# Up projection: the first 256 columns of u and g on tokens 0 to 255 first, the last 128 tokens afterwards with tokens stationary

## The chip, the cores and the metric

The kernel runs on one core of one Trainium2 chip. The metric is the device time of one execution in microseconds (us), lower is better; the time before is the median of three runs.

## The reference

One layer of a hybrid trunk: adaptive layer norm, a mixer of retention and mLSTM heads, its output projection, a post-norm, and then a feed-forward block with a convolution over tokens. It works on 384 tokens (128 of a prompt, 256 of a latent grid whose rows are 64 wide), with a model width of 2048 and a feed-forward width `D_FF` of 5504. All values are float32. The part around the change:

```python
x = _ln(ALPHA * x + g1 * mix) * ln1_g + ln1_b      # mix = heads @ w_out
h = _ln(x) * (1.0 + sc2) + sh2
...
ug = h @ w_up                                      # (tokens, 2 * D_FF)
u, g = ug[..., :D_FF], ug[..., D_FF:]
ffn = (silu(_seq_conv(u, conv_ff, grid)) * g) @ w_down
...
x = _ln(ALPHA * x + g2 * ffn) * ln2_g + ln2_b
```

`_seq_conv` takes, for each column, a weighted sum over three neighbouring tokens, within the prompt or within a grid row. g2 is one of six modulation vectors, each a product of a conditioning vector with a slice of `w_mod`.

## The kernel before, in words

**Arithmetic.** Every float32 operand of a product is split into two fp32r parts, hi (a cast on ACT, L117) and lo (source minus hi, on DVE or POOL, L118). A product is three matmuls: hi·hi, hi·lo, lo·hi. Tokens come in three tiles of 128: tile 0 is the prompt, tiles 1 and 2 the latent grid. The width of 2048 is 16 k-tiles.

**The stages around the change.** The output projection `w_out` is done in four blocks of 512 columns. The last block goes token tile by token tile, each followed by `norms(tt)`: residual, post-norm (DVE, L945 and L947, 128x2048 each), statistics (bn_stats, L1027), the negative scaled mean nm (L927, with a power on POOL that gives brs), and the normalised rows xn on ACT (L1033; for tile 2 the rows lie in the buffer l1g, for tile 0 in g1b). Then `h2_piece(tt, kt)` turns a 128x128 piece of xn by a PE transpose (L114, tile xtp), scales and shifts it to h (ACT L1048 for single pieces of tiles 0 and 1, DVE L1050 else) and splits it: ah on ACT, al on POOL (single pieces of tiles 0 and 1) or DVE. After five k-tiles, tiles 1 and 2 go together, as pieces of 256 tokens.

The up projection has the columns stationary and the tokens moving: `mm_a` (L182 to L184) multiplies a 128x128 block of weights with all 384 tokens, N = 384. It works on 256 columns at a time, first of u, then of g; the product's sums are the PSUM tiles psu. The first u product runs inside the stage of the h2 pieces, two pieces behind; the first g product is `up_product(pmm, 1, 0, 2)`. `up_gate` then makes the gated activation: ACT writes y = u times the middle convolution weight (L1120, scale from cfw), DVE adds the two outer taps from u in PSUM (`conv_taps`, four instructions L345 and L349 for each 128 columns), ACT applies silu (L1122), DVE multiplies by g (L1123), and the result is split into fah and fal for the down projection.

cfw holds the convolution's weights. They are loaded by POOL's DMA queue as rows (cfr, L1097), transposed on PE (pcf) and copied on DVE (cfw, L1102). The last modulation vector, g2's, is accumulated on DVE in the feed-forward stage: for each of 16 k-tiles and each half, SP loads 128x1024 weights (mraw, L234, three buffers) and DVE does a pair of instructions on macc (L283 for the first k-tile, L286 after), one for each conditioning vector.

**What sets the order.** The framework schedules every instruction from dependencies and its own estimates, and fixes for each engine and each DMA queue one order, which the engine follows in order. Buffers come from pools, and later pools take over the space of earlier ones; an instruction that writes a buffer waits for the last reader of what lay there before. Weights go through four raw buffers (SP, L141), and three hi and lo buffers each. PSUM has eight banks: five of pool pmm and three of pool pat in the stage of the change, and from the third product on eight of pool pps, in the same space. The next u product (columns 256 to 511) thus reuses banks of the stage before.

Of the kernel before, what the change touches and what calls it, by code (L numbers as in the profile page):

```python
# [9 lines left out]
F32 = mybir.dt.float32  # L10
F32R = mybir.dt.float32r
# [4 lines left out]
P = 128  # L16
D = 2048
KT = D // P
LP = 128
LS = 256  # L20
T = LP + LS
# [61 lines left out]
def hybrid_step(ctx, tc, ca, cb, x_prompt, x_sample, state_ret, state_c, state_n, state_m, c, c_ctx,  # L83
# [74 lines left out]
    def weights_a(w2, k0, nk, c0, nc_=256, perm=False):  # L158
        src = w2[k0 * P:(k0 + nk) * P, c0:c0 + nc_].rearrange("(k p) n -> p k n", p=P)
        return weights([(lambda r: r[:, :nk * nc_].rearrange("p (k n) -> p k n", k=nk), src)], nk * nc_, perm)  # L160
# [18 lines left out]
    def mm_a(ps, w, kk, width, m, ah, al, start, stop):  # L179
        hi, lo = w  # L180
        s = slice(kk * width + m * P, kk * width + (m + 1) * P)
        nc.tensor.matmul(ps, lhsT=hi[:, s], rhs=ah, start=start, stop=False)  # L182
        nc.tensor.matmul(ps, lhsT=hi[:, s], rhs=al, start=False, stop=False)  # L183
        nc.tensor.matmul(ps, lhsT=lo[:, s], rhs=ah, start=False, stop=stop)  # L184
# [765 lines left out]
    with ExitStack() as p2:  # L950
        g1p = pool("g1p", 1, p2, reuse_waits="tile")
        sb2 = pool("sb2", 2, p2, reuse_waits="tile")
        g1b = g1p.tile([P, 2, D], F32, name="g1b")
        l1g = g1p.tile([P, D], F32, name="l1g")
        l1b = g1p.tile([P, D], F32, name="l1b")
        for kt in range(KT - 2, KT):
            new_act(kt, mixt[kt])
        mixs.close()
        share_splits(0)
        xnp = pool("xnp", 1, p2, side="right", reuse_waits="tile")  # L960
        wo = w_out[0]
        p2m = ExitStack()
        mp = pool("mp2", 3, p2m, reuse_waits="tile")
        raws4 = mod_loads(lambda: mp.tile([P, 2048], F32, tag="mraw", name="mraw"),
                          [(q, 4, 4 * D + j * 512, 512) for j in range(2 * NV, 4) for q in range(0, KT, 4)], 2)
        mods4 = Stepper(chain(*[mod_tensor(4, 4 * j, 4, pmm, sb2, raws4, 4) for j in range(2 * NV, 4)]), 0.9)

        def residual_loads(nb):
            s = slice(nb * 512, (nb + 1) * 512)
            for tt in range(NT):  # L970
                nc.sync.dma_start(out=r[tt][:, s], in_=tok_rows(x_prompt, x_sample, tt)[:, s])
            for v in range(2):
                nc.sync.dma_start(out=g1b[:, v, s], in_=modrow[2, v:v + 1, s].to_broadcast([P, 512]))

        def w_out_block(nb, ks):
            ps = [(pat if nb == 1 else pmm).tile([P, 512], F32, tag="ps", name="pso") for _ in range(NT)]
            for k0 in range(0, ks, 2):
                part_b(ps, weights_b(wo, k0, 2, (nb * 512,)), 2, k0, 0, KT - 1)
                if nb > 0:
                    mods4.step()  # L980
                if nb < 3 and k0 == 10:
                    residual_loads(nb)
                if nb == 2 and k0 == 14:
                    residual_loads(3)
                if nb == 1 and k0 == 8:
                    mod_from_rows(3, KT, pat, sb2, "sh2", 0.0)
                if nb == 2 and k0 == 6:
                    rows_bcast(l1g, ln1_g, D)
                    rows_bcast(l1b, ln1_b, D)
                if nb == 2 and k0 == 8:  # L990
                    mod_from_rows(4, 8 * NV, pat, sb2, "sc2", 1.0)
            return ps

        for nb in range(3):
            ps = w_out_block(nb, KT)
            for tt in range(NT):
                residual(sb2, g1b, tt, nb, ps[tt], True, True)
        mods4.finish()
        p2m.close()
        wx = pool("wx", 1, p2, reuse_waits="tile")  # L1000
        ps = [pmm.tile([P, 512], F32, tag="ps", name="pso") for _ in range(NT)]
        ws = []
        for i in range(KT // 2):
            raw = wraw.tile([P, 1024], F32, tag="raw", name="raw")
            nc.sync.dma_start(out=raw.rearrange("p (k n) -> p k n", k=2),
                              in_=wo[2 * i * P:(2 * i + 2) * P, 1536:2048].rearrange("(k p) n -> p k n", p=P))
            if i < KT // 2 - 3:
                hi = wx.tile([P, 1024], F32R, name=f"wxh{i}")
                lo = wx.tile([P, 1024], F32R, name=f"wxl{i}")
                split(hi, lo, raw)  # L1010
                ws.append((hi, lo))
            else:
                ws.append(split_weights(raw))
        xn = [None] * NT

        def norms(tt):
            residual(sb2, g1b, tt, 3, ps[tt], True, True)
            if tt == NT - 1:
                mark["pb1"] = mark["pow"]
            st = post_stats(tt)  # L1020
            if tt == NT - 1:
                mark["pa2"] = mark["pow"]
            for s in post_norm(tt, st, l1g, l1b, 1):
                pass
            xst = small.tile([P, 4, 6], F32, tag="bst", name="xst")
            for j in range(4):
                nc.vector.bn_stats(out=xst[:, j, :], in_=r[tt][:, j * 512:(j + 1) * 512])  # L1027
            mv, rs = aggr(xst)
            nm = neg_scaled_mean(mv, rs)
            t = l1g if tt == NT - 1 else g1b[:, 0, :] if tt == 0 else xnp.tile([P, D], F32, tag="xn", name="xn")  # L1030
            for j in range(4):
                s = slice(j * 512, (j + 1) * 512)
                nc.scalar.activation(t[:, s], r[tt][:, s], AF.Identity, bias=nm, scale=rs)  # L1033
            xn[tt] = t

        new_hi, new_lo = [None] * KT, [None] * KT

        def h2_piece(tt, kt, n=1):
            w = n * P
            ps = pat.tile([P, w], F32, tag="ps", name="xtp")  # L1040
            for j in range(n):
                transpose(ps[:, j * P:(j + 1) * P], xn[tt + j][:, kt * P:(kt + 1) * P])
            ts = slice(tt * P, tt * P + w)
            h = sb2.tile([P, 2 * P], F32, tag="h2", name="h2", bufs=5)[:, :w]
            v = min(tt, 1)
            sc, sh = modf["sc2"][:, v, kt:kt + 1], modf["sh2"][:, v, kt:kt + 1]
            if tt < 2 and n == 1:
                nc.scalar.activation(h, ps, AF.Identity, bias=sh, scale=sc)  # L1048
            else:
                nc.vector.tensor_scalar(out=h, in0=ps, scalar1=sc, scalar2=sh, op0=ALU.mult, op1=ALU.add)  # L1050
            if tt == 0:
                new_hi[kt] = acts.tile([P, T], F32R, tag=f"ah{kt}", name=f"ah{kt}")
                new_lo[kt] = acts.tile([P, T], F32R, tag=f"al{kt}", name=f"al{kt}")
            split(new_hi[kt][:, ts], new_lo[kt][:, ts], h, nc.gpsimd if tt < 2 and n == 1 else nc.vector)

        for tt in range(NT):
            for kt in range(KT):
                mm_b(ps[tt], ws[kt // 2], kt % 2, act_hi[kt], act_lo[kt], tt, kt == 0, kt == KT - 1)
                if tt == NT - 1 and kt >= 5:
                    h2_piece(0, kt - 5)  # L1060
            norms(tt)
        for kt in range(KT - 5, KT):
            h2_piece(0, kt)
        for kt in range(5):
            h2_piece(1, kt)
        wu, wd = w_up[0], w_down[0]
        ps_first = [pmm.tile([P, T], F32, tag="ps", name="psu") for _ in range(2)]
        wg = None
        for i in range(KT + 2):
            if i < 5:  # L1070
                h2_piece(2, i)
            elif i < KT:
                h2_piece(1, i, 2)
            if i == KT - 1:
                mark["h2"] = mark["lo"]
            kt = i - 2
            if kt < 0:
                continue
            if kt % 4 == 0:
                if kt < 12:  # L1080
                    with tc.issue_after(mark["pb1"] if kt < 4 else mark["pa2"]):
                        wg = weights_a(wu, kt, 4, 0, 256)
                else:
                    wg = weights_a(wu, kt, 4, 0, 256)
            for m in range(2):
                mm_a(ps_first[m], wg, kt % 4, 256, m, new_hi[kt], new_lo[kt], kt == 0, kt == KT - 1)
        act_hi[:], act_lo[:] = new_hi, new_lo


# [37 lines left out]
            out.append((ah, al))  # L1127
        return out

    a = up_gate(0, ps_first, up_product(pmm, 1, 0, 2))  # L1130
    psum_a.close()
    pps = pool("pps", 8, p3, space=PSUM, reuse_waits="tile")

# [116 lines left out]
```

## Time and profile before

| what | us |
|---|---|
| runs: median of three (lowest, highest) | 2064.02 (2063.2, 2068.23) |
| the profiled execution's own time | 2066.45 |
| its span | 2064.6 |
| PE busy in the span | 1985.1 (96%) |
| DVE busy | 1238.6 (60%) |
| ACT busy | 688.5 (33%) |
| POOL busy | 235.9 (11%) |
| mean granted TensorE clock (share of full speed) | 0.984 |

Busy times are sums over an engine's instructions. The chain is the work that ended last, followed back from the last instruction, each step to what released it. Rows of a timeline give start, duration, engine, line of the kernel, operation and tiles (out<-in), and in brackets the idle time of the engine just before and what ended it. Matmuls are pipelined, so their spacing from start to start, not the duration, tells what one costs. The granted clock (PEclk) is the TensorE clock that the throttle gave, as a share of full speed.

### The profile page before, as it was taken

What the parts mean: (1) busy time and instruction counts of PE and PEld (TensorE: products, weight loads), DVE (VectorE), ACT (ScalarE), POOL (GpSimd) and SP (SyncE); (2) the same over time, 40 slices, a digit from 0 to 9 for tenths busy, and PEclk for the clock granted to TensorE, in tenths of its full rate; (3) what the DMA queues carried; (4) which work ended last, traced back from release to release, by engine and by line L of the source; (5) the groups of instructions that cost most, each with busy time, mean ns of one, the idle gap of its engine ahead of it and who ended that gap; (6) DMA issues with size and microseconds to landing.
All of it is one profiled execution on the core that took longest, in us unless ns stands there. A gap on an engine that the chain in (4) does not pass through costs nothing.

```text
span 2064.6 us, 26331 instructions
## 1 busy us (share of the span) xinstructions
PE 1985.1 (96%) x10233; PEld 1748.3 (85%) x10233; DVE 1238.6 (60%) x1792; ACT 688.5 (33%) x1048; POOL 235.9 (11%) x225
## 2 busy tenths in 40 slices
PE   6999999999989998998999999999999999999995
PEld 4677888898878876777999889999889998999984
DVE  4655798987879744477944323477334444444478
ACT  4223333333333443235233333333222332233331
POOL 0001354222212111022000000000000000000004
PEclk9999999999999999998999999999999999999998
DMA  9895985876877436734744334465334444434342
GB/s 348 262 307 167 183 202 173 257 204 215 197 186 221 142 104 222 278 111 137 246 123 123 125 129 124 123 202 181 123 130 124 123 143 143 127 109 143 113 153 102
DMA packets 260637, 352.30 MB, mean 171 GB/s; under 512 B 16143, under 2 KB 200784, under 8 KB 259360
## 3 DMA queue, kind: packets, MB, share of 16 engines
q1 hardware_dynamic: 256240, 340.08, 55.0%
q0 software_dynamic: 4272, 10.54, 1.5%
q8 instruction: 80, 1.31, 0.3%
q14 instruction: 45, 0.37, 0.0%
HBM read 343.16 MB, written 7.41 MB: 170 GB/s over the span
## 4 chain that ended last, share of the span: by engine, by line
PE 82%; DVE 9%; DMA 3%; issue 3%; SPq 1%; POOL 1%; ACT 1%; POOLq 0%; DVEq 0%; ACTq 0%
PE psu L182 11%; PE psu L184 11%; PE psu L183 11%; PE psd L192 5%; PE psd L191 5%; PE psd L190 5%; DVE macc L286 4%; PE psa L182 3%; PE psa L184 3%; PE psa L183 3%; PE psb L191 3%; PE psb L190 3%; PE psb L192 3%; DMA mraw<-in_w_mod 2%; PE pso L190 2%
## 5 line engine op out<-in xcount | busy, mean ns | idle before, releaser
L118 DVE TENSOR_TENSOR lo<-raw,hi 128x1024 fp32r<-128x1024 f32 (+4 forms) x444 | 486.3, 1101 | 533.4 <-ACT hi L117 533.0
L117 ACT CAST hi<-raw 128x1024 fp32r<-128x1024 f32 (+4 forms) x473 | 434.9, 929 | 941.0 <-PE psu L183 355.7
L183 PE MATMUL psu<-al,hi 128*128 128x384 f32 x1376 | 467.4, 340 | 0.0
L184 PE MATMUL psu<-ah,lo 128*128 128x384 f32 x1376 | 464.2, 339 | 2.7 <-DVE lo L118 2.7
L182 PE MATMUL psu<-ah,hi 128*128 128x384 f32 x1376 | 466.3, 340 | 0.0
L286 DVE SCALAR_TENSOR_TENSOR macc<-mraw,ct,macc 128x1024 f32<-128x1024 f32 x210 | 285.4, 1396 | 16.1 <-DMA mraw<-in_w_mod 16.0
L184 PEld LDWEIGHTS psu<-ah,lo 128*128 128x128 f32 x1376 | 258.8, 188 | 3.0 <-DVE lo L118 3.0
L182 PEld LDWEIGHTS psu<-ah,hi 128*128 128x128 f32 x1376 | 258.9, 188 | 1.9 <-issue 0.8
L183 PEld LDWEIGHTS psu<-al,hi 128*128 128x128 f32 x1376 | 259.0, 188 | 0.2
L192 PE MATMUL psd<-hi,fal 128*128 128x512 f32 (+1 forms) x484 | 192.0, 397 | 0.0
L191 PE MATMUL psd<-lo,fah 128*128 128x512 f32 (+1 forms) x484 | 189.8, 392 | 0.0
L190 PE MATMUL psd<-hi,fah 128*128 128x512 f32 (+1 forms) x484 | 186.7, 390 | 0.0
L182 PE MATMUL psa<-ah,hi 128*128 128x384 f32 x512 | 177.5, 351 | 1.7 <-ACT hi L117 1.7
L184 PE MATMUL psa<-ah,lo 128*128 128x384 f32 x512 | 176.4, 346 | 1.6 <-DVE lo L118 1.5
L183 PE MATMUL psa<-al,hi 128*128 128x384 f32 x512 | 176.4, 345 | 0.0
L191 PE MATMUL psb<-lo,ah 128*128 128x512 f32 x384 | 154.3, 402 | 1.1 <-DVE lo L118 1.1
L192 PE MATMUL psb<-hi,al 128*128 128x512 f32 x384 | 152.8, 398 | 0.0
L190 PE MATMUL psb<-hi,ah 128*128 128x512 f32 x384 | 146.7, 401 | 1.7 <-ACT hi L117 1.7
L182 PEld LDWEIGHTS psa<-ah,hi 128*128 128x128 f32 x512 | 96.7, 190 | 16.8 <-issue 9.1
L191 PEld LDWEIGHTS psd<-lo,fah 128*128 128x128 f32 x484 | 90.9, 188 | 23.2
L190 PEld LDWEIGHTS psd<-hi,fah 128*128 128x128 f32 x484 | 90.9, 188 | 21.1
L192 PEld LDWEIGHTS psd<-hi,fal 128*128 128x128 f32 x484 | 90.9, 188 | 20.6
(301 smaller groups left out, 2241.4 us busy)
## 6 DMA issues: line engine op xcount, KB each, us to landing
raw<-in_w_up SPq DMA_DIRECT2D x168, 512.0 KB, 3.8
mraw<-in_w_mod SPq DMA_DIRECT2D x112, 512.0 KB, 5.0
raw<-in_w_down SPq DMA_DIRECT2D x84, 512.0 KB, 3.6
raw<-in_w_in SPq DMA_DIRECT2D x128, 256.0 KB, 4.6
raw<-in_w_in SPq DMA_DIRECT2D x52, 512.0 KB, 6.5
wm<-in_w_mod SPq DMA_DIRECT2D x20, 1024.0 KB, 9.2
raw<-in_w_out SPq DMA_DIRECT2D x32, 512.0 KB, 4.1
wm<-in_w_mod SPq DMA_DIRECT2D x16, 768.0 KB, 6.8
```

The lines of the kernel that those rows point to most:

```text
L117: nc.scalar.copy(dst_hi, src)
L118: mark["lo"] = (eng or nc.vector).tensor_tensor(out=dst_lo, in0=src, in1=dst_hi.bitcast(F32), op=ALU.subtract).ins
L182: nc.tensor.matmul(ps, lhsT=hi[:, s], rhs=ah, start=start, stop=False)
L183: nc.tensor.matmul(ps, lhsT=hi[:, s], rhs=al, start=False, stop=False)
L184: nc.tensor.matmul(ps, lhsT=lo[:, s], rhs=ah, start=False, stop=stop)
L190: nc.tensor.matmul(ps, lhsT=ah[:, t], rhs=hi[:, s], start=start, stop=False)
L191: nc.tensor.matmul(ps, lhsT=ah[:, t], rhs=lo[:, s], start=False, stop=False)
L192: nc.tensor.matmul(ps, lhsT=al[:, t], rhs=hi[:, s], start=False, stop=stop)
L286: nc.vector.scalar_tensor_tensor(out=acc[:, v, :], in0=raw, scalar=ct[:, kt, v:v + 1], in1=acc[:, v, :], op0=ALU.mult, op1=ALU.add)
```

## The change

Before, the first u product waits piece by piece for h2 of all three token tiles, and the first g product follows as a product of its own. After, both are started together on tiles 0 and 1 alone:

- Four PSUM tiles `early` (u and g, 128 columns each). The loop over 16 k-tiles makes an h2 piece of tile 1 (single, on ACT and POOL) and runs `mm_a` for u and g on 256 tokens, N = 256: 192 matmuls. From k-tile 8 on it also makes two pieces of tile 2 (on DVE).
- The eight weight loads (four groups of four k-tiles, u and g) are kept: five pairs of hi and lo go into the `wx` buffers that held weights of `w_out` (tiles wuh and wul), three into the ordinary hi and lo buffers. The marks that held back the first weight loads (`issue_after`) are gone.
- Tile 2 follows with its tokens stationary: 96 matmuls of 128x128 tokens against 256 columns of weights, N = 256, into the PSUM tile `psl`, first g, then u, the k-groups in the order 3, 2, 1, 0. ACT copies the two results to rows (tile `late`), and four PE transposes put them into the last 128 columns of the `early` tiles.
- `up_gate(0, *early)` follows; the separate first g product is gone.

Lines behind the new code move by 15 (L1123 is then L1138, L1102 is L1117, L1097 is L1112).

```diff
-                hi = wx.tile([P, 1024], F32R, name=f"wxh{i}")
-                lo = wx.tile([P, 1024], F32R, name=f"wxl{i}")
+                hi = wx.tile([P, 1024], F32R, name=f"wxh{i}", tag=f"wxh{i}")
+                lo = wx.tile([P, 1024], F32R, name=f"wxl{i}", tag=f"wxl{i}")
...
-            if tt == NT - 1:
-                mark["pb1"] = mark["pow"]
             st = post_stats(tt)
-            if tt == NT - 1:
-                mark["pa2"] = mark["pow"]
...
-        for kt in range(5):
+        wu, wd = w_up[0], w_down[0]
+        early = [[pmm.tile([P, T], F32, tag="ps", name="psu") for _ in range(2)] for _ in range(2)]
+        ws_up = {}
+        for kt in range(KT):
+            if kt % 4 == 0:
+                for ug in range(2):
+                    raw = wraw.tile([P, 1024], F32, tag="raw", name="raw")
+                    nc.sync.dma_start(out=raw.rearrange("p (k n) -> p k n", k=4),
+                                      in_=wu[kt * P:(kt + 4) * P, ug * DFF:ug * DFF + 256]
+                                      .rearrange("(k p) n -> p k n", p=P))
+                    i = kt // 2 + ug
+                    if i < 5:
+                        hi = wx.tile([P, 1024], F32R, name=f"wuh{i}", tag=f"wxh{i}")
+                        lo = wx.tile([P, 1024], F32R, name=f"wul{i}", tag=f"wxl{i}")
+                        split(hi, lo, raw)
+                        ws_up[kt // 4, ug] = hi, lo
+                    else:
+                        ws_up[kt // 4, ug] = split_weights(raw)
             h2_piece(1, kt)
-        wu, wd = w_up[0], w_down[0]
-        ps_first = [pmm.tile([P, T], F32, tag="ps", name="psu") for _ in range(2)]
-        wg = None
-        for i in range(KT + 2):
-            if i < 5:
-                h2_piece(2, i)
-            elif i < KT:
-                h2_piece(1, i, 2)
...
-            if kt % 4 == 0:
-                if kt < 12:
-                    with tc.issue_after(mark["pb1"] if kt < 4 else mark["pa2"]):
-                        wg = weights_a(wu, kt, 4, 0, 256)
-                else:
-                    wg = weights_a(wu, kt, 4, 0, 256)
+            if kt >= 8:
+                h2_piece(2, 2 * kt - 16)
+                h2_piece(2, 2 * kt - 15)
+            for ug in range(2):
+                for m in range(2):
+                    mm_a(early[ug][m][:, :2 * P], ws_up[kt // 4, ug], kt % 4, 256, m,
+                         new_hi[kt][:, :2 * P], new_lo[kt][:, :2 * P], kt == 0, kt == KT - 1)
+        late = pat.tile([P, 2, 256], F32, tag="ps", name="psl")
+        ts = slice(2 * P, T)
+        for ug in (1, 0):
+            for n, kt in enumerate([kt for kg in (3, 2, 1, 0) for kt in range(4 * kg, 4 * kg + 4)]):
+                hi, lo = ws_up[kt // 4, ug]
+                cols = slice(kt % 4 * 256, kt % 4 * 256 + 256)
+                for a, b in ((new_hi, hi), (new_hi, lo), (new_lo, hi)):
+                    nc.tensor.matmul(late[:, ug, :], lhsT=a[kt][:, ts], rhs=b[:, cols],
+                                     start=n == 0 and b is hi and a is new_hi, stop=n == KT - 1 and a is new_lo)
+        rows = sb2.tile([P, 512], F32, tag="rt", name="late")
+        for ug in (1, 0):
+            nc.scalar.copy(rows[:, ug * 256:ug * 256 + 256], late[:, ug, :])
+        for ug in (1, 0):
             for m in range(2):
-                mm_a(ps_first[m], wg, kt % 4, 256, m, new_hi[kt], new_lo[kt], kt == 0, kt == KT - 1)
+                c0 = ug * 256 + m * P
+                transpose(early[ug][m][:, ts], rows[:, c0:c0 + P])
...
-    a = up_gate(0, ps_first, up_product(pmm, 1, 0, 2))
+    a = up_gate(0, *early)
```

**DVE, tile 1's normalisation.** r_6697 and r_6698 are the residual rows of tiles 1 and 2, xst the statistics of the normalised rows, bmv their aggregate, lo and wul weight splits. Before, from tile 1's post-norm to its nm (the last row):

```order
L947 SCALAR_TENSOR_TENSOR r_6697<-r_6697,brs,l1b 128x2048
L1027 BN_STATS xst<-r_6697 128x6 x4
L118 TENSOR_TENSOR lo<-raw,hi 128x1024
L210 BN_AGGR bmv<-xst 128x2
L118 TENSOR_TENSOR lo<-raw,hi 128x1024
L916 TENSOR_TENSOR rtmp<-pso,g1b 128x512
L198 TENSOR_SCALAR veps<-bmv 128x1
L118 TENSOR_TENSOR lo<-raw,hi 128x1024
L918 SCALAR_TENSOR_TENSOR r_6698<-r_6698,rtmp 128x512
L927 SCALAR_TENSOR_TENSOR nm<-bmv,brs 128x1
```

After, the same stretch begins one weight split earlier; its first twelve rows:

```order
L118 TENSOR_TENSOR wul_7875<-raw,wuh_7874 128x1024
L947 SCALAR_TENSOR_TENSOR r_6697<-r_6697,brs,l1b 128x2048
L118 TENSOR_TENSOR wul_7881<-raw,wuh_7880 128x1024
L118 TENSOR_TENSOR wul_7959<-raw,wuh_7958 128x1024
L118 TENSOR_TENSOR wul_7965<-raw,wuh_7964 128x1024
L1023 BN_STATS xst<-r_6697 128x6 x4
L118 TENSOR_TENSOR wul_8043<-raw,wuh_8042 128x1024
L916 TENSOR_TENSOR rtmp<-pso,g1b 128x512
L118 TENSOR_TENSOR lo<-raw,hi 128x1024
L210 BN_AGGR bmv<-xst 128x2
L918 SCALAR_TENSOR_TENSOR r_6698<-r_6698,rtmp 128x512
L118 TENSOR_TENSOR lo<-raw,hi 128x1024
```

Five weight splits more stand there, ahead of tile 1's nm; a third lo and rows of tile 2 follow before nm itself.

**DVE, the end of the first products.** cfw is the copy of the convolution's weights, macc the modulation vector's accumulation, L345 and L349 the taps. Before:

```order
L283 TENSOR_SCALAR macc<-mraw,ct 128x1024 x2
L1102 COPY cfw<-pcf 128x129
L286 SCALAR_TENSOR_TENSOR macc<-mraw,ct,macc 128x1024 x2
L118 TENSOR_TENSOR lo<-raw,hi 128x1024
L286 SCALAR_TENSOR_TENSOR macc<-mraw,ct,macc 128x1024 x2
L345 SCALAR_TENSOR_TENSOR y<-psu,cfw,y 128x127
L349 SCALAR_TENSOR_TENSOR y<-psu,cfw,y 128x4x63
L118 TENSOR_TENSOR lo<-raw,hi 128x1024
```

After:

```order
L118 TENSOR_TENSOR lo<-raw,hi 128x1024 x3
L283 TENSOR_SCALAR macc<-mraw,ct 128x1024 x2
L286 SCALAR_TENSOR_TENSOR macc<-mraw,ct,macc 128x1024 x2
L1117 COPY cfw<-pcf 128x129
L286 SCALAR_TENSOR_TENSOR macc<-mraw,ct,macc 128x1024 x2
L345 SCALAR_TENSOR_TENSOR y<-psu,cfw,y 128x127
L349 SCALAR_TENSOR_TENSOR y<-psu,cfw,y 128x4x63
L345 SCALAR_TENSOR_TENSOR y<-psu,cfw,y 128x127
L349 SCALAR_TENSOR_TENSOR y<-psu,cfw,y 128x4x63
L286 SCALAR_TENSOR_TENSOR macc<-mraw,ct,macc 128x1024 x2
```

Three lo splits of the next u product's weights now stand ahead of the first macc, and one macc pair more ahead of cfw. Behind the last row come four more tap rows, a macc pair, the two products with g (L1138), a pair, the two fal splits, five macc instructions and the next u's fourth lo split.

**SP's queue, the loads behind the first weights of the up projection.** Before:

```order
L1005 DMA raw<-in_w_out 128x2x512 x8
L141 DMA raw<-in_w_up 128x4x256 x9
L234 DMA mraw<-in_w_mod 128x1024 x3
L141 DMA raw<-in_w_up 128x4x256
L234 DMA mraw<-in_w_mod 128x1024 x2
```

After:

```order
L1005 DMA raw<-in_w_out 128x2x512 x8
L1067 DMA raw<-in_w_up 128x4x256 x8
L141 DMA raw<-in_w_up 128x4x256 x7
L234 DMA mraw<-in_w_mod 128x1024 x11
L141 DMA raw<-in_w_up 128x4x256
```

The first mraw load now stands behind fifteen w_up loads instead of nine, the last of which takes the raw buffer of the next u product's third weights. The buffer of the first mraw lies where wul of the third k-group of u (wul_8043) was, which the late block reads.

On POOL, cfr's load stood ahead of all the al splits and now stands behind all 32 of tiles 0 and 1; its buffer lies where wuh_7958 was, whose last reader has twelve matmuls of the late block behind it. On PE, the transposes of cfr (pcf) stood in the middle of the first products. Now they are the last rows before the next u product, whose matmuls begin with the fourth row from the end here:

```order
L1093 MATMUL psl<-wuh_7874,ah_7716 128x256
L1093 MATMUL psl<-wul_7875,ah_7716 128x256
L1093 MATMUL psl<-wuh_7874,al_7717 128x256
L114 MATMUL psu<-cst,late 128x128 x4
L114 MATMUL pcf<-cst,cfr 128x43 x3
L182 MATMUL psu<-ah_7683,hi 128x384
L183 MATMUL psu<-al_7684,hi 128x384
L184 MATMUL psu<-ah_7683,lo 128x384
L182 MATMUL psu<-ah_7683,hi 128x384
```

The first of these psu matmuls writes the bank of the second column tile of the first u, so it waits for the last tap that reads it (L349), in both kernels.

More of the change, by code (lines that the diff above doesn't have):

```diff
@@ L1063, in hybrid_step @@
             h2_piece(0, kt)
-        for kt in range(5):
-            h2_piece(1, kt)
-        wu, wd = w_up[0], w_down[0]
-        ps_first = [pmm.tile([P, T], F32, tag="ps", name="psu") for _ in range(2)]
-        wg = None
-        for i in range(KT + 2):
-            if i < 5:
-                h2_piece(2, i)
-            elif i < KT:
-                h2_piece(1, i, 2)
[L1074 to L1078, printed above, removed]
-            if kt % 4 == 0:
-                if kt < 12:
-                    with tc.issue_after(mark["pb1"] if kt < 4 else mark["pa2"]):
-                        wg = weights_a(wu, kt, 4, 0, 256)
-                else:
-                    wg = weights_a(wu, kt, 4, 0, 256)
+        wu, wd = w_up[0], w_down[0]
```

## The prediction

> **What bounds the kernel now.** I read the page first, then the table of stretches around the change, then the timelines of PE, DVE, ACT and SP in it, then the DMA view. The chain that ended last is PE's work for the most part:
>
> ```profile
> PE 82%; DVE 9%; DMA 3%; issue 3%; SPq 1%; POOL 1%; ACT 1%; POOLq 0%; DVEq 0%; ACTq 0%
> ```
>
> So a change pays only where PE stands still, and what it adds to PE it costs. The stretches (columns: window, length, PE busy (count), PEld, DVE, ACT, POOL, granted clock, DMA share, GB/s) show where PE stands still: in the first, between the last product of the output projection and the first of the up projection, thirty instructions, all but one transposes, in 19.7 us; the second holds the first u and g products, the third and fourth the u product of columns 256 to 511 (here "the next u").
>
> ```profile
> 922.40:942.10 19.70, 9.33 (x30) 4.57 (x29) 15.95 (x29) 17.61 (x50) 14.78 (x23) 0.63 0.31 95
> 942.10:979.50 37.40, 37.40 (x213) 36.82 (x212) 29.50 (x50) 14.65 (x24) 0.00 (x0) 0.97 0.56 172
> 979.50:992.40 12.90, 12.90 (x74) 12.90 (x74) 12.90 (x14) 4.60 (x7) 0.00 (x0) 1.00 0.73 235
> ...
> 995.00:1000.00 5.00, 4.54 (x17) 4.54 (x18) 5.00 (x5) 0.00 (x0) 0.00 (x0) 0.66 0.85 230
> ```
>
> The timeline of PE has the ends of these stretches (start, duration, engine, line, operation). The first product starts at 942.12, its 192 matmuls (counted by the row of the psu tiles alone) end where the next u starts, at 979.51, without a gap. The next u stands from 992.41 to 995.46 for its fourth lo split on DVE and then runs cold:
>
> ```profile
> 942.12 0.99 PE L182 MATMUL psu<-ah,hi 128*128 128x384 f32 x2
> ...
> 979.51 0.34 PE L182 MATMUL psu<-ah,hi 128*128 128x384 f32 x1
> ...
> 992.41 0.34 PE L183 MATMUL psu<-al,hi 128*128 128x384 f32 x1
> 995.46 0.45 PE L184 MATMUL psu<-ah,lo 128*128 128x384 f32 x1 [2.71 <-DVE lo L118]
> ...
> 999.39 0.34 PE L182 MATMUL psu<-ah,hi 128*128 128x384 f32 x1
> ```
> ```profile
> 942.10:979.50 37.40, 36.95 (x192) 34.67 (x193) 2.86 (x8) 1.17 (x2) 0.97 0.56 172
> ```
>
> **The streaming, part by part.** Warm spacings, start to start, come from these rows: the first two are seven starts of a dense run (six spacings, 1.06 us: 0.1767 us at N = 384), the next two are 23 starts (22 spacings, 2.64 us: 0.120 at N = 256, from the last down product), the last two four transposes (0.11 each).
>
> ```profile
> 957.20 0.34 PE L182 MATMUL psu<-ah,hi 128*128 128x384 f32 x1
> ...
> 958.26 0.34 PE L182 MATMUL psu<-ah,hi 128*128 128x384 f32 x1
> ```
> ```profile
> 2040.17 0.28 PE L191 MATMUL psd<-lo,fah 128*128 128x256 f32 x1
> ...
> 2042.81 0.28 PE L192 MATMUL psd<-hi,fal 128*128 128x256 f32 x1
> ```
> ```profile
> 953.54 0.27 PE L114 MATMUL xtp<-cst,xn 128*128 128x128 f32 x1
> ...
> 953.87 0.27 PE L114 MATMUL xtp<-cst,l1g 128*128 128x128 f32 x1
> ```
>
> Removed: 192 x 0.1767 = 33.9. Added: 192 + 96 matmuls at N = 256, 288 x 0.120 = 34.6. The arithmetic itself costs 0.7. Between them stay about 27 transposes (3.0; the 16 of tile 2 and the 11 of tile 1 that now stand among the matmuls) and a cold start. The clock's price is read off the stall: from 995.46 to 999.39 are 13 spacings, 3.93 us for 13 x 0.1767 = 2.30, so 1.6 lost. The block from first early matmul to last late one is 34.6 + 3.0 + 1.6 = 39.2 us.
>
> The Trainium skill, "TensorE: Matmul & The Clock Gate", section "Wait — 56ns, not 53.3ns?", gives N ÷ 2.4 GHz plus about 2.5 ns for warm back-to-back matmuls, 109 ns at N = 256: by that the 288 would take 31.4 us, and the end would come 3.2 us earlier than below. This trace's 0.120 is for the same operand type and width, so the row decides.
>
> **The head.** The early matmuls need only tile 1's normalised rows, not tile 2's. On DVE three weight splits stand ahead of tile 1's nm before; with the change five more (the wul tiles) do, about 1.2 each by these rows (DVE first, then ACT, which makes the rows from nm):
>
> ```profile
> 921.29 1.21 DVE L118 TENSOR_TENSOR lo<-raw,hi 128x1024 fp32r<-128x1024 f32 x1
> ...
> 922.59 1.16 DVE L118 TENSOR_TENSOR lo<-raw,hi 128x1024 fp32r<-128x1024 f32 x1
> ...
> 924.32 1.22 DVE L118 TENSOR_TENSOR lo<-raw,hi 128x1024 fp32r<-128x1024 f32 x1
> ...
> 926.86 0.41 DVE L927 SCALAR_TENSOR_TENSOR nm<-bmv,brs 128x1 f32<-128x1 f32 x1 [0.46 <-POOL brs L200]
> ...
> 938.00 0.41 DVE L927 SCALAR_TENSOR_TENSOR nm<-bmv,brs 128x1 f32<-128x1 f32 x1 [0.84 <-POOL brs L200]
> ```
> ```profile
> 928.17 2.92 ACT L1033 ACTIVATE xn<-r,nm,brs 128x512 f32<-128x512 f32 x4
> ...
> 938.44 2.93 ACT L1033 ACTIVATE l1g<-r,nm,brs 128x512 f32<-128x512 f32 x4 [0.30 <-DVE nm L927]
> ```
>
> Tile 1's nm becomes 926.9 + 5 x 1.2 = 932.9. From nm to the first product tile 2 takes 942.1 − 938.0 = 4.1 now; tile 1's nm waited 0.9 longer for ACT than tile 2's did (1.3 against 0.4), so the first early matmul is at 932.9 + 4.1 + 0.9 = 937.9, not 942.1. Bounds: 932 if the five splits were hidden, 942 if their loads are late. I take 937.9, since the order on DVE puts all five ahead. The late block then ends at 937.9 + 39.2 = 977.1 instead of 979.5: 2.4 gained. The row copies on ACT and four transposes (0.44 on PE) lie under the wait that follows, at no cost; without that wait they would cost about 1.2.
>
> **The tail: what the next u waits for.** Here the change adds a wait. The weights' third hi and lo buffers are read in the late block until its 60th matmul, 36 before the end: 977.1 − 36 x 0.12 = 972.8. Then the next u's third weights are split, hi on ACT and lo on DVE; I take the lo's 1.2 above for each: 975.2. Only then its raw buffer is free, SP gets past that w_up load, and behind it come all the mraw loads of the modulation vector, the first of which also needs a buffer that the late block reads. Before, they went out at 955. The DMA view has their landing and that of cfr, and POOL's row where cfr is issued:
>
> ```profile
> 955.05 5.96 SPq L234 DMA_DIRECT2D mraw<-in_w_mod  x3
> ```
> ```profile
> mraw<-in_w_mod SPq DMA_DIRECT2D x19, 512.0 KB, 4.5
> ...
> mbt<-in_b_mod POOLq DMA_DIRECT2D x2, 128.0 KB, 2.8
> cfr<-in_conv_ff POOLq DMA_DIRECT2D x1, 64.5 KB, 7.4
> ```
> ```profile
> 916.38 1.91 POOL L1097 DMA_DIRECT2D cfr<-in_conv_ff  x1
> ```
>
> The first mraw goes out at about 975.3 and lands at 979.8; the second, 0.52 MB at the 235 GB/s of the third stretch, 2.2 later, at 982.0. On DVE two macc pairs, which need these two, now stand ahead of the cfw copy, and further pairs between the convolution taps. Each step's price:
>
> ```profile
> 963.40 1.41 DVE L283 TENSOR_SCALAR macc<-mraw,ct 128x1024 f32<-128x1024 f32 x2
> 964.72 0.29 DVE L1102 COPY cfw<-pcf 128x129 f32<-128x129 f32 x1
> 964.92 2.47 DVE L286 SCALAR_TENSOR_TENSOR macc<-mraw,ct,macc 128x1024 f32<-128x1024 f32 x2
> 967.31 1.22 DVE L118 TENSOR_TENSOR lo<-raw,hi 128x1024 fp32r<-128x1024 f32 x1
> ...
> 970.84 0.35 DVE L345 SCALAR_TENSOR_TENSOR y<-psu,cfw,y 128x127 f32<-128x127 f32 x1
> ...
> 971.48 1.22 DVE L118 TENSOR_TENSOR lo<-raw,hi 128x1024 fp32r<-128x1024 f32 x1
> ...
> 977.69 0.48 DVE L349 SCALAR_TENSOR_TENSOR y<-psu,cfw,y 128x252 f32<-128x252 f32 x1
> ...
> 981.60 0.56 DVE L1123 TENSOR_TENSOR y<-y,psu 128x384 f32<-128x384 f32 x1
> ...
> 986.05 0.57 DVE L118 TENSOR_TENSOR fal<-y,fah 128x384 fp32r<-128x384 f32 x1
> ...
> 988.18 6.09 DVE L286 SCALAR_TENSOR_TENSOR macc<-mraw,ct,macc 128x1024 f32<-128x1024 f32 x5
> 994.16 1.24 DVE L118 TENSOR_TENSOR lo<-raw,hi 128x1024 fp32r<-128x1024 f32 x1
> ```
>
> A macc pair is 2.4, cfw 0.2, four tap rows 2 x 0.64 = 1.3 (start to start). From 982.0: pair 984.4, cfw 984.6, pair 987.0, four taps 988.3, pair 990.7, four taps 991.9. The next u's first matmul writes the bank that the last tap reads, so it starts at 992.0. Before, the last tap ended at 978.2, ahead of 979.51, and the bank was free. cfr isn't what binds: its buffer is read until 12 matmuls before the late block's end, so it lands between 975.7 + 2.8 = 978.5 and 975.7 + 7.4 = 983.1, and three short transposes (under 0.4) later cfw could run, before its turn at 984.4. ACT's y lies under the pair behind cfw.
>
> The fourth lo split, for which the next u stands now, comes after a pair (994.3), two L1123 products (995.4), a pair (997.8), two fal splits (998.9), five macc (6.0: 1004.9): it ends at 1006.2. It is needed 12.9 after the start plus 1.6 for the cold clock: 1006.5. The old stall just goes.
>
> **The sum.** Before, the next u ends at 979.5 + 96 x 0.1767 + 2.9 (3.05 less one spacing) + 1.6 = 1001.0. After: 992.0 + 17.0 + 1.6 = 1010.6. Behind that the chain is PE's products one after the other, with no gap in which the delay could be made up, so 9.6 us stay. The profiled execution took 2066.45 (span 2064.6), 2.4 above the median of the runs, 2064.02; the difference carries over: 2076.0 for a profiled execution, and 2064.0 + 9.6 = **2073.6 us**.
>
> The Trainium skill, same page, section "What's actually happening", has the clock halve after an idle window of about 3.4 us. Here the granted clock was 0.66 after a gap of 2.7. By the page's window before's stall would not have cooled PE by itself, and its going would give back 1.6 less, 11.2 in the sum; the row decides.
>
> **The rivals.**
> - *The loads are not held (not slower).* Place: SP's first mraw and POOL's cfr. If their buffers don't bind and both have landed when DVE finishes the third lo at 975.2, then DVE runs 1.3 + 2.4 + 0.2 + 2.4 + 1.3 + 2.4 + 1.3 = 11.3 without a wait, the next u starts at 986.5 and ends at 1005.1: 4.1 more, 2068.1, no difference that counts. It decides at a first mraw landed by 975. For it: SP ran these loads 20 us ahead before. Against: eleven stand behind the w_up loads in SP's order. Chance 0.12.
> - *The stall stays as well.* The fourth lo has 0.3 us to spare. If the mraw loads come at more than 2.4 apart, every macc between waits, and the next u stands twice: 2 to 4 more, 2075.6 to 2077.6. For it: DMA is at 235 GB/s there, and the eleven mraw and five w_up loads of that stage want 8.4 MB, 36 us at that rate. Against: DVE had no gap for a load from 979.5 to 992.4 (12.90 of 12.90 busy). Chance 0.17.
> - *The head does not come earlier (the change does not do what it says).* If the eight early loads or the splits push tile 1's chain to 937, the early matmuls start at 942.1 and everything moves by 4.2: 2077.8. Chance 0.12.
> - *Faster.* It would need the third lo some 16 us earlier, or the taps done before the late block is; nothing in the rows allows that. Chance 0.04.
>
> **How the numbers follow.** My forecast keeps 0.55, with 2070.5 to 2077 as its own range (the head's start 3 us to either side). 0.3% is 6.2 us, about what a measurement of this kernel can tell from no change (the three runs before lie 5.0 apart). Within it: the first rival and a small part of the forecast's low end, 0.14. Faster 0.04. Slower 0.82. The range, 2067 to 2080, takes in the first rival's 2068.1 and both dearer ones; it leaves out the faster case and sums of two dear cases.
>
> **What would show it.** Right: the first early matmul near 938, the late block's end near 977, then PE idle for some 14 us but for seven transposes, its releaser DVE's taps (or cfr's landing for the first part of it); DVE idle before the first macc for DMA mraw; the next u from 992, cold at first, with no gap before its fourth lo. Wrong: a next u that starts before 987; a first early matmul at or after 942; cfr landing after 985; or a gain in a later stage, for which I see no cause.

## The result and the profile after

The changed kernel takes 2082.36 us (median of four runs, 2078.83 to 2084.21), the kernel before 2063.61 (four runs, 2062.69 to 2068.23). That is 18.8 us slower, where 9.6 was forecast and the range ended at 2080. The ratio is 1.0084 (95% interval 1.0064 to 1.0105); it goes by the means of the same runs, 2081.9 and 2064.5, which are 17.4 apart. The profiled execution after has a span of 2081.1, the one before 2064.6.

PE has nearly the same work; its busy time is 1987.3 against 1985.1, and its share of the chain fell. From the page of after:

```profile
PE 1987.3 (95%) x10333; PEld 1751.9 (84%) x10333; DVE 1236.9 (59%) x1792; ACT 693.8 (33%) x1072; POOL 247.3 (12%) x236
...
PE 78%; DVE 11%; DMA 4%; issue 3%; SPq 1%; POOL 1%; ACT 1%; POOLq 0%; DVEq 0%; ACTq 0%
...
L182 PE MATMUL psu<-ah,hi 128*128 128x384 f32 (+1 forms) x1336 | 449.8, 339 | 7.8 <-DVE y L349 7.8
```

Before, PE's idle time among the up projection's matmuls was 2.7 us, for a lo split (L184); now it is 7.8 us ahead of an L182 matmul, and a convolution tap ends it. The stretches (PE busy in the third column) place it: the early and late block, the wait, and the first part of the next u.

```profile
937.00:978.60 41.60, 40.12 (x315) 39.44 (x314) 20.00 (x43) 18.22 (x51) 10.41 (x18) 0.92 0.10 28
978.60:997.70 19.10, 1.48 (x9) 0.80 (x8) 11.54 (x18) 2.35 (x5) 2.09 (x3) 0.66 0.70 211
997.70:1012.40 14.70, 14.63 (x73) 14.67 (x74) 14.70 (x15) 4.77 (x8) 0.00 (x0) 0.87 0.53 174
```

In the middle one PE does 1.5 us of work in 19.1. Its timeline names what it waits for, twice in a row: first for cfr, then for the last tap.

```profile
978.53 0.28 PE L1093 MATMUL psl<-wuh,al 128*128 128x256 f32 x1
979.27 0.72 PE L114 MATMUL psu<-cst,late 128*128 128x128 f32 x4 [0.46 <-ACT late L1097]
989.38 0.55 PE L114 MATMUL pcf<-cst,cfr 43*128 43x43 f32 x3 [9.39 <-DMA cfr<-in_conv_ff]
997.76 0.66 PE L182 MATMUL psu<-ah,hi 128*128 128x384 f32 x1 [7.84 <-DVE y L349]
```

DVE in the same time: it stands for the first mraw (5.10), does two macc pairs, stands again, now for pcf (4.11), and then goes through pair, taps, pair, taps. The last tap starts at 997.15, and PE goes on right behind it.

```profile
975.73 1.23 DVE L118 TENSOR_TENSOR lo<-raw,hi 128x1024 fp32r<-128x1024 f32 x1 [3.02 <-ACT hi L117]
982.05 1.42 DVE L283 TENSOR_SCALAR macc<-mraw,ct 128x1024 f32<-128x1024 f32 x2 [5.10 <-DMA mraw<-in_w_mod]
983.38 2.47 DVE L286 SCALAR_TENSOR_TENSOR macc<-mraw,ct,macc 128x1024 f32<-128x1024 f32 x2
989.96 0.29 DVE L1117 COPY cfw<-pcf 128x129 f32<-128x129 f32 x1 [4.11 <-PE pcf L114]
990.17 2.47 DVE L286 SCALAR_TENSOR_TENSOR macc<-mraw,ct,macc 128x1024 f32<-128x1024 f32 x2
...
993.85 2.47 DVE L286 SCALAR_TENSOR_TENSOR macc<-mraw,ct,macc 128x1024 f32<-128x1024 f32 x2
...
997.15 0.47 DVE L349 SCALAR_TENSOR_TENSOR y<-psu,cfw,y 128x252 f32<-128x252 f32 x1
...
1010.16 1.22 DVE L118 TENSOR_TENSOR lo<-raw,hi 128x1024 fp32r<-128x1024 f32 x1
```

The executions differ by some us ahead of this stage, so times of different kernels are compared from one mark, the start of the last matmul of the output projection (922.24 before, 920.58 after). From it the next u starts at 57.3 before and 77.2 after, and the first down product at 231.4 and 248.6: 17.2 later. From there to the end of the span they take 911.0 and 911.9.

### The profile page after: what moved, and what is told of

It is laid out like the page before. It is cut to its first block, busy times and chain, and to the rows that moved or that the text cites. A ratio compares the mean times of both kernels' runs of the same rounds, so it can differ in the third digit from the quotient of the medians.

```text
span 2081.1 us, 26570 instructions
## 1 busy us (share of the span) xinstructions
PE 1987.3 (95%) x10333; PEld 1751.9 (84%) x10333; DVE 1236.9 (59%) x1792; ACT 693.8 (33%) x1072; POOL 247.3 (12%) x236
## 4 chain that ended last, share of the span: by engine, by line
PE 78%; DVE 11%; DMA 4%; issue 3%; SPq 1%; POOL 1%; ACT 1%; POOLq 0%; DVEq 0%; ACTq 0%
PE psu L183 12%; PE psu L182 12%; PE psu L184 12%; PE psd L192 5%; PE psd L191 5%; PE psd L190 5%; DVE macc L286 4%; PE psa L182 3%; PE psa L183 3%; PE psa L184 3%; PE psb L191 2%; PE psb L192 2%; PE psb L190 2%; PE modps L255 2%; PE pso L190 2%
## 5 line engine op out<-in xcount | busy, mean ns | idle before, releaser
L118 DVE TENSOR_TENSOR lo<-raw,hi 128x1024 fp32r<-128x1024 f32 (+4 forms) x439 | 479.5, 1098 | 537.7 <-ACT hi L117 537.3
L117 ACT CAST hi<-raw 128x1024 fp32r<-128x1024 f32 (+4 forms) x468 | 429.6, 927 | 941.9 <-PE psu L183 356.6
L182 PE MATMUL psu<-ah,hi 128*128 128x384 f32 (+1 forms) x1336 | 449.8, 339 | 7.8 <-DVE y L349 7.8
L183 PE MATMUL psu<-al,hi 128*128 128x384 f32 (+1 forms) x1336 | 451.2, 338 | 0.0
L184 PE MATMUL psu<-ah,lo 128*128 128x384 f32 (+1 forms) x1336 | 448.8, 338 | 0.0
L182 PEld LDWEIGHTS psu<-ah,hi 128*128 128x128 f32 x1336 | 250.2, 188 | 9.8 <-issue 8.8
L183 PEld LDWEIGHTS psu<-al,hi 128*128 128x128 f32 x1336 | 251.3, 188 | 0.1
L184 PEld LDWEIGHTS psu<-ah,lo 128*128 128x128 f32 x1336 | 251.1, 188 | 0.0
L182 PE MATMUL psa<-ah,hi 128*128 128x384 f32 x512 | 177.8, 352 | 1.7 <-ACT hi L117 1.7
L184 PE MATMUL psa<-ah,lo 128*128 128x384 f32 x512 | 176.3, 346 | 1.6 <-DVE lo L118 1.5
L182 PEld LDWEIGHTS psa<-ah,hi 128*128 128x128 f32 x512 | 96.8, 190 | 16.8 <-issue 9.1
```

What stands on the lines that cost most here:

```text
L117: nc.scalar.copy(dst_hi, src)
L118: mark["lo"] = (eng or nc.vector).tensor_tensor(out=dst_lo, in0=src, in1=dst_hi.bitcast(F32), op=ALU.subtract).ins
```

## The experiments

**Theory A**: the loss is PE's wait between the late block and the next u, and the wait has three causes one behind the other: cfr lands late, macc stands ahead of cfw and the taps, and the next u's first matmul needs the bank that the last tap reads. **Theory B**: the loss is work of PE's own (N = 256, the late block, the transposes), and a shorter wait would be made up elsewhere. All kernels change the changed kernel, except the one that changes the kernel before. The medians are set beside those of the kernel before on the same chip, and the ratios go by the means.

| kernel | median | before | ratio, 95% interval | next u from the mark | first down product |
|---|---|---|---|---|---|
| after | 2082.36 | 2063.61 | 1.0064 to 1.0105 | 77.2 | 248.6 |
| macc behind the taps | 2078.03 | 2064.68 | 1.0050 to 1.0080 | 72.1 | 244.4 |
| that, mraw loads held | 2072.25 | 2064.68 | 1.0023 to 1.0051 | 68.8 | 240.7 |
| cfr early | 2070.33 | 2064.68 | 1.0022 to 1.0044 | 65.5 | 237.5 |
| cfr early, macc behind | 2068.94 | 2065.39 | 1.0005 to 1.0023 | 63.7 | 235.5 |
| free banks alone | 2084.09 | 2064.68 | 1.0073 to 1.0107 | 57.9 | 248.6 |
| no wait (all three) | 2071.75 | 2065.39 | 1.0021 to 1.0046 | 58.3 | 237.6 |
| no wait, splits behind nm | 2072.41 | 2065.39 | 1.0021 to 1.0043 | 58.6 | 237.9 |
| no wait, macc later | 2063.64 | 2065.14 | 0.9984 to 1.0002 | 58.2 | 229.1 |
| before, macc behind the taps | 2060.71 | 2065.39 | 0.9972 to 0.9990 | | 226.8 |

**cfr early.** The load goes ahead of the early block, into columns of g1b that are free:

```diff
+        cfr = g1b[:NF, 1, :3 * P].rearrange("f (t p) -> f t p", t=3)
+        nc.gpsimd.dma_start(out=cfr, in_=conv_ff[0].rearrange("t (f p) -> f t p", p=P))
...
-    cfr = sb3.tile([NF, 3, P], F32, tag="y", name="cfr")
-    nc.gpsimd.dma_start(out=cfr, in_=conv_ff[0].rearrange("t (f p) -> f t p", p=P))
```

> After with the load of cfr moved ahead of the al splits of tile 1, into a buffer that is free there (columns of g1b that tile 2's residual has read); in the order this brings cfw and three of the four tap rows ahead of the first macc. Theory A (the loss is PE's wait before the next u: late cfr, macc ahead of cfw and taps): pcf inside the late block, the next u starts at about 984 instead of 997.8, the fourth lo at 998 is in time, the total falls by 13 to 14, to about 2069. Theory B (the loss is PE's own added work, N = 256 and the late block, and the wait would be made up elsewhere): the next u may start earlier, the total stays above 2077.

It came to 2070.33, 12 less than after, close to the 13 to 14 of theory A. These columns had been read long before, so cfr went out at 827.9 already. The next u started 65.5 after the mark, not at about 63: the last tap rows still stood behind the first macc, which waited for its mraw. On DVE, and what PE then waited for:

```profile
985.70 1.41 DVE L283 TENSOR_SCALAR macc<-mraw,ct 128x1024 f32<-128x1024 f32 x2 [0.93 <-DMA mraw<-in_w_mod]
987.03 0.34 DVE L345 SCALAR_TENSOR_TENSOR y<-psu,cfw,y 128x127 f32<-128x127 f32 x1
987.30 0.47 DVE L349 SCALAR_TENSOR_TENSOR y<-psu,cfw,y 128x252 f32<-128x252 f32 x1
```
```profile
987.91 0.66 PE L182 MATMUL psu<-ah,hi 128*128 128x384 f32 x1 [5.71 <-DVE y L349]
```

**macc behind the taps.** Every macc instruction is ordered behind the last tap of the first columns, that of `up_gate(0)`:

```diff
+            mark["tap"] = tap.ins
...
             if f0 >= 4:
-                mods5.step()
+                with tc.issue_after(mark["first"]):
+                    mods5.step()
...
+    mark["first"] = mark["tap"]
```

> After with all macc instructions ordered behind the last tap of the first columns, cfr as late as in after. Theory A: cfr lands where it did, near 989.4, cfw 990, the taps end without macc pairs between them at 993.4, the next u starts there instead of 997.8: 4.4 less, about 2078. If the taps' wait is only what shows and the fourth lo (behind macc) is the true bound, no gain: 2082.

2078.03, 4.3 less, as theory A said. The two macc pairs between cfw and the last tap were gone, so that from cfw to the next u it took 3.8 instead of 7.8; cfr landed only 1.0 earlier from the mark than in after.

**The mraw loads held as well.** On top of the edit before, the first mraw load goes behind one more load of w_up on SP's queue (`mark["ld"]` is the latest such load):

```diff
+            if f0 == 2 and ug == 1 and k0 == 12:
+                mark["ld8"] = mark["ld"]
             if f0 >= 4:
-                with tc.issue_after(mark["first"]):
+                with tc.issue_after(mark["first"]), tc.issue_after(mark["ld8"]):
...
```

> As the kernel with macc behind the taps, and the mraw loads also ordered behind one more w_up load on SP's queue, so that no mraw load is under way while cfr is. Theory A1 (cfr landed after 11.6 us because three mraw loads of 0.52 MB went out 0.3 us before it): it lands within 7.4 us or less, by 985, and the next u starts near 988.5: 9 less, about 2073. Theory A2 (the queue of POOL is slow by itself there): it lands 11 to 12 us after its issue, and the time is that of the kernel with macc behind the taps, about 2078.

2072.25, 10 less than after, and A1 is right. cfr's row in the DMA view (last number: us from issue to landing) of after, of the kernel with macc behind the taps, and of this one:

```profile
cfr<-in_conv_ff POOLq DMA_DIRECT2D x1, 64.5 KB, 11.6
```
```profile
cfr<-in_conv_ff POOLq DMA_DIRECT2D x1, 64.5 KB, 10.5
```
```profile
cfr<-in_conv_ff POOLq DMA_DIRECT2D x1, 64.5 KB, 7.5
```

With three mraw loads under way cfr takes 10.5; in after, where two more go out before it lands (at 983.5 and 985.9), 11.6; with none, 7.5, near the 7.4 of the kernel before. The load is the same in all three, and so is the rest of its company: a w_up load issued 0.7 before it, and two mbt loads behind it on POOL's queue.

**cfr early and macc behind the taps.** Both edits above.

> After with cfr early and all macc behind the last tap of the first columns. In the kernel with cfr early alone the last two tap rows still stood behind two macc instructions that waited for their mraw. Theory A: without these the taps end about 2.4 earlier, the next u starts 63 us after the last output-projection matmul (65.5 with cfr early alone, 77.2 in after, 57.3 before): 2.4 less than with cfr early alone, about 2068, still 3 to 4 slower than before. Theory B (what is left over before is not this wait): no change from 2070.

2068.94; the next u starts at 63.7 from the mark, near the 63 and 2068 expected. What is left of the wait is the path from the late block's end over the row copies, four transposes, ACT's y and eight tap rows to the bank.

**Free banks alone.** The next u's tiles come from the pools of the stage before:

```diff
+    us2 = up_product(None, 0, 2, 2, [p_.tile([P, T], F32, tag="ps", name="psu") for p_ in (pmm, pat)])
     psum_a.close()
...
-            us = up_product(pps, 0, f, m)
+            us = us2 if f == 2 else up_product(pps, 0, f, m)
```

> After with the next u product in two PSUM banks that the taps do not read (the fifth bank of the first pool and one of the second), so that its first matmul waits for no tap; the order also moves its fourth lo ahead of most macc. Theory A: the next u starts right behind pcf, at 989.9, and runs through: 7.9 less, about 2074.5. Theory B: no change beyond 2 us.

Theory A's expectation failed: 2084.09, nothing gained, as theory B had it, though the next u started right behind the late block and stood only 4.7 us for cfr in its midst. The time was taken back further on. The next weights' loads stand behind mraw loads on SP's queue, and these wait for macc, which began as late as in after (61.2 from the mark, 61.5 there). PE stood twice in the second g product, and its first down product began at 248.6 as in after. The second of these waits is for a lo split behind seven macc instructions (PE first, then DVE):

```profile
1016.53 0.69 PE L182 MATMUL psu<-ah,hi 128*128 128x384 f32 x1 [3.87 <-ACT hi L117]
...
1024.48 0.69 PE L184 MATMUL psu<-ah,lo 128*128 128x384 f32 x1 [6.94 <-DVE lo L118]
```
```profile
1014.84 8.45 DVE L286 SCALAR_TENSOR_TENSOR macc<-mraw,ct,macc 128x1024 f32<-128x1024 f32 x7
1023.21 1.21 DVE L118 TENSOR_TENSOR lo<-raw,hi 128x1024 fp32r<-128x1024 f32 x1
```

So the bank is only the wait that shows; behind it DVE's queue is a bound of its own, about as late.

**No wait: all three causes taken away.** cfr early, macc behind the taps, free banks.

> The kernel before this one with the next u in banks that the taps don't read as well, so all three causes of the wait are gone. Theory A: the next u follows the late block without a gap, 58 us after the last output-projection matmul, in time with before (57.3), and before's own stall (3.05 and a cold clock) is not there: 2062 to 2064, no slower than before. Theory B: N = 256, the late block and the transposes cost PE time of their own: 2067 or more.

Missed: 2071.75, not 2062 to 2064. The next u did follow the late block without a gap (58.3 from the mark). But the order now had eight macc instructions ahead of the last lo of the second g product, and PE stood there. PE first, then DVE:

```profile
1010.45 0.34 PE L183 MATMUL psu<-al,hi 128*128 128x384 f32 x1
1017.29 0.69 PE L184 MATMUL psu<-ah,lo 128*128 128x384 f32 x1 [6.50 <-DVE lo L118]
```
```profile
1006.44 9.66 DVE L286 SCALAR_TENSOR_TENSOR macc<-mraw,ct,macc 128x1024 f32<-128x1024 f32 x8
1016.00 1.23 DVE L118 TENSOR_TENSOR lo<-raw,hi 128x1024 fp32r<-128x1024 f32 x1
```

This number alone would have spoken for theory B. The trace shows a wait of the same kind at another place: a lo split behind macc.

**No wait, macc later.** On top of the kernel without the wait, macc is held behind the last tap of the second columns:

```diff
             out += up_gate(f, us, up_product(pps, 1, f, m))
+            if f == 2:
+                mark["first"] = mark["tap"]
```

> As the kernel without the wait (cfr early, macc held, free banks), with macc held behind the last tap of the second columns instead of the first. In the kernel without the wait PE stood 6.84 us for the last lo of the second g product, which stood behind eight macc instructions. Theory A (PE's own work of the change costs little; what is lost is waits for DVE's macc and for cfr): that stall goes with its cold clock (1.6), the first down product begins 229 to 230 us after the last output-projection matmul (231.4 before, 237.6 in the kernel without the wait), 2062 to 2064, no slower than before but slower than the kernel before with macc behind the taps (2060.7). Theory B (the stall moves once more, to a later weight): 2067 or more.

2063.64, ratio 0.9984 to 1.0002: no difference from before. In the next u and the second g product PE waits only once more, for 0.55:

```profile
1006.25 0.44 PE L184 MATMUL psu<-ah,lo 128*128 128x384 f32 x1 [0.55 <-DVE lo L118]
```

Of the 18.8 us nothing is left, and no work of PE was changed; theory B falls as the explanation of the loss. A small rest isn't excluded: the kernel before has a stall of its own, and beside it with that stall removed (the last experiment) the first down product comes 2.3 later here, and the ratios 0.9993 and 0.9981 are some 2.5 us apart, though their intervals overlap.

**No wait, the splits behind tile 1's nm.** Made on the kernel without the wait, to ask whether the five splits cost the head its gain:

```diff
-                        split(hi, lo, raw)
+                        with tc.issue_after(mark["nm1"]) if kt else ExitStack():
+                            split(hi, lo, raw)
...
```

> As the kernel without the wait, and the weight splits of all but the first two early loads ordered behind tile 1's nm on DVE, so that six splits less stand ahead of it. Theory A (the splits delay the head): the first early matmul comes at 12 to 12.5 us after the last output-projection matmul instead of 16.4, the late block ends 4 earlier, 2058 to 2060. Rival (the early block is then paced by tile 1's pieces on ACT and POOL): it starts earlier and ends no earlier, 2062 to 2064.

Neither number came: 2072.41, with the 6.84 us stall of the kernel without the wait still in it, so the place of the first early matmul is what tells. Tile 1's nm came at 928.17, 4.3 from the mark instead of 11.8, but the first early matmul at 17.4 instead of 16.4. The rival of this experiment is nearer: PE waits for tile 1's pieces, ACT's h among them waits for POOL's al splits, and these come one behind the other without a pause. Here is nm of after, then of this kernel, then ACT's h and POOL's splits of tile 0's last and tile 1's first pieces:

```profile
932.34 0.41 DVE L927 SCALAR_TENSOR_TENSOR nm<-bmv,brs 128x1 f32<-128x1 f32 x1 [0.68 <-POOL brs L200]
```
```profile
928.17 0.41 DVE L928 SCALAR_TENSOR_TENSOR nm<-bmv,brs 128x1 f32<-128x1 f32 x1 [0.64 <-POOL brs L200]
```
```profile
939.19 0.46 ACT L1048 ACTIVATE h<-xtp,sh,sc 128x128 f32<-128x128 f32 x1 [1.37 <-POOL al L118]
```
```profile
931.32 2.52 POOL L200 TENSOR_TENSOR brs<-veps,mhalf 128x1 f32<-128x1 f32 x1 [1.29 <-DVE veps L198]
933.82 11.55 POOL L118 TENSOR_TENSOR al<-h,ah 128x128 fp32r<-128x128 f32 x14
```

Fourteen al splits take 11.55. That isn't 0.83 for each: nine of them take about 0.45, as one does with DVE idle (after, 946.14: 0.47), and five take 1.06 to 2.50. A long one stands beside a DVE instruction with two inputs in SBUF, the post-norm here; beside bn_stats, which has one, four take 1.69 (POOL first, then DVE):

```profile
936.65 2.50 POOL L118 TENSOR_TENSOR al<-h,ah 128x128 fp32r<-128x128 f32 x1
...
941.91 1.69 POOL L118 TENSOR_TENSOR al<-h,ah 128x128 fp32r<-128x128 f32 x4
```
```profile
936.22 2.62 DVE L949 SCALAR_TENSOR_TENSOR r<-r,brs,l1b 128x2048 f32<-128x2048 f32 x1
...
941.55 2.46 DVE L1025 BATCH_NORM_STATS2 xst<-r 128x6 f32<-128x512 f32 x4
```

The Trainium skill, "SBUF — State Buffer", section "Who interferes with whom", says that a DVE instruction with two SBUF inputs contends with a GpSimd instruction that reads SBUF, and that the second one blocks until the first is done; the trace agrees, 2.50 beside the post-norm against 0.45 beside bn_stats. That POOL now holds the head is read off these waits; no run without them was made.

**The kernel before, macc behind the taps.** The same hold, nothing else.

> The kernel before the change, with all macc behind the last tap of the first columns and nothing else. Theory A: the fourth lo of the next u no longer stands behind five macc instructions, the stall of 3.05 us at 992.41 and its cold clock (1.6) go: 4.5 less, about 2060. If the stall is only moved to a later weight: 2063 to 2065.

2060.71, ratio 0.9981 (0.9972 to 0.9990): the expected 4.5 came (4.7 by the medians). The idle time of L184, 2.7 us before, is gone from the page:

```profile
L184 PE MATMUL psu<-ah,lo 128*128 128x384 f32 x1376 | 463.2, 339 | 0.0
```

It is the fastest of all, faster than both kernels, and 2.9 faster than the best version with the change.

## Why the prediction was wrong, point by point

The direction was right, and so was the end of the path: PE waits ahead of the next u, the taps release it, and macc stands ahead of cfw and between the taps. The forecast has about half of the loss. The step that failed is that cfr doesn't bind: in the trace cfr, and not the first macc pairs, is what cfw waits for last. The other half of the miss is the block, taken 2.5 us too short and begun 0.8 too early.

- **Head.** Forecast 937.9, which is 15.7 from the mark; measured 936.99, 16.4 from the mark. Right within 0.8, but the reason was incomplete: with six splits fewer ahead of nm the head gains nothing, since POOL's al splits are next late, and slow beside some of DVE's instructions.
- **The block.** Forecast 39.2, measured 936.99 to 978.65: 41.7. The streaming was right (36 matmuls from 974.45 to 978.65, 0.117 each; 0.120 was taken). The Trainium skill's 109 ns ("TensorE: Matmul & The Clock Gate", section "Wait — 56ns, not 53.3ns?") is below it, as the row before had said. Most of the difference lies at the block's start: the first al matmuls waited 1.15 for POOL, and PE ran cold until 943.6, 6.6 us after its first matmul (granted clock 0.50 from 937 to 943; 0.21 from start to start, 0.12 behind it). These first 6.7 us hold 23 matmuls, 2.8 us at 0.120, so nearly 4 us were lost where 1.6 was allowed. About 0.7 more went at 951, where six transposes took 1.35 with a wait for ACT among them. The block's start:

```profile
936.99 1.22 PE L182 MATMUL psu<-ah,wuh 128*128 128x256 f32 x4
939.36 0.58 PE L183 MATMUL psu<-al,wuh 128*128 128x256 f32 x1 [1.15 <-POOL al L118]
...
943.58 0.30 PE L183 MATMUL psu<-al,wuh 128*128 128x256 f32 x1
```

  So the first u and g were not done 2.4 earlier, but 0.8 later than before (58.1 against 57.3 from the mark). The early start bought nothing.
- **cfr: the step that failed.** "cfr isn't what binds: ... it lands between ... 978.5 and ... 983.1 ..., before its turn at 984.4." It landed at 989.4, 11.6 after its issue, outside both ends, and past the 985 that the prediction named as a sign of being wrong. The bounds were rows of loads that had the queues nearly to themselves, while the same prediction put three mraw loads of 0.52 MB at that very time on SP's queue. The experiment with the mraw loads held shows that they are the cause: after 7.5 cfr would have been there at 985.2, ahead of DVE. DVE was ready for cfw at 985.8 and began it at 989.96: 4.1 us.
- **mraw.** Forecast 979.8, measured 982.05 (from the mark 57.6 and 61.5), mostly since the block ended 3.2 later; the landing took 4.6, where 4.5 was taken. It came before cfr and cost nothing beyond it.
- **Pairs and taps.** From the start of cfw to the next u 7.6 forecast (984.4 to 992.0), 7.8 measured (989.96 to 997.76).
- **The fourth lo.** Done at 1011.4, needed at 997.76 + 14.5 = 1012.3: in time, as forecast. The old stall went.
- **The sum.** 9.6 + 3.2 (block's end, 58.1 for 54.9 from the mark) + 4.1 (cfr) + 0.2 (pairs and taps) gives 17.1; the traces have 17.2.
- **Rivals.** The loads were held: cfr's waited for the late block, and SP's first mraw went out at 977.4. The stall for the fourth lo did not come in after; it came only in experiments, where the next u had been freed. The head came earlier (16.4 from the mark, 19.9 before), so that rival fell as well.

The medians have 18.8, the means 17.4, the two traces 17.2 in this stage and 16.5 in their spans. These differences lie within the spread of the runs (5.5 between the four of the kernel before), and aren't explained further.

What stays open is whether the head could be made earlier with the al splits off POOL. It wasn't tried, since DVE, the other engine for them, has tile 2's post-norm in the same time.

## What to carry to other kernels

When a product is moved ahead, look at what the order lets slip behind it: a small load whose buffer is now read longer, and filler work (here macc) that the order puts into the place where the old product hid it. A landing time is a row of its company: take it from a place with the same loads under way, or bound it from above by adding theirs (here 7.4 for cfr and 6.7 for three mraw loads at the prediction's 235 GB/s, an estimate of 14.1; 10.5 to 12.5 were measured). Where one wait is removed and nothing is gained, look for the next late thing on the same queue before the theory is dropped: here it took four removals until the 18.8 us were back. And try the smallest edit on the kernel before first; holding the filler work there was worth more than the change.

## What the runs showed of the hardware

- A 64.5 KB load on POOL's queue took 7.4 us in the kernel before, where DMA moved under 30 GB/s. It took 7.5 with a 0.52 MB load issued 0.7 us before it on SP's queue, 10.5 with three more issued 0.3 us before it, and 11.6 and 12.5 where another two followed before it landed (after, and free banks alone). While the 10.5 passed DVE stood idle.
- A POOL subtraction of 128x128 took 0.45 to 0.47 us with DVE idle or in bn_stats, and up to 2.50 beside DVE instructions with two operands in SBUF.
- Warm 128x256 fp32r matmuls followed one another at 0.117 to 0.120 us; after the gap of 7.84 us PE ran at 0.32 per 128x384 matmul from 998.2 to 1001.4, then at 0.176.
